# The steps of a forward substitution, written for VectorE and for GpSimd

## The chip, the cores and the metric

The kernel runs on one core of a Trainium2 chip. The metric is the device time of one execution in microseconds, and the median of the runs shown counts. Engines are named as the profile names them: PE (TensorE, with PEld for its weight loads), DVE (VectorE), ACT (ScalarE), POOL (GpSimd) and SP (SyncE, here a queue of DMAs).

## The reference

One layer of a hybrid decoder over 512 positions and 2048 channels. Half of the channels are 16 heads of a delta-rule recurrence, the other half pooled windows. Then follow an output projection, a gated embedding and a norm:

```python
h = rms_norm(x, norm_g[i])
z = jnp.einsum('btd,dn->btn', h, w_in[i])      # r, k, v, lora, gates, pool input
...
def step(S, inp):
    r_t, w_t, k_t, v_t, kk_t, a_t = inp
    sa = jnp.einsum('bhvk,bhk->bhv', S, -kk_t)
    S = (S * w_t[:, :, None, :]
         + sa[..., None] * (kk_t * a_t)[:, :, None, :]
         + v_t[..., None] * k_t[:, :, None, :])
    y_t = jnp.einsum('bhvk,bhk->bhv', S, r_t)
    return S, y_t
...
x = x + jnp.einsum('btc,cd->btd', y_mix, w_out[i])
gate = jax.nn.sigmoid(jnp.einsum('btd,de->bte', x, w_pg[i]) + b_pg[i])
x = x + gate * jnp.einsum('btq,qd->btd', p[i], w_ple[i])
```

All data is float32.

## The kernel before

Every large product is done three times with operands split into a high and a low part: a weight piece is loaded into `raw` by a DMA on SP's queue, ScalarE casts it to `whi`, VectorE subtracts to `wlo` (lines 127 to 134), and TensorE multiplies (`mm3`, line 164). There are four buffers of each, so a load can only start when the `wlo` of four pieces earlier is done, and SP issues its DMAs strictly in the order in which they stand on its queue.

The recurrence goes in eight pairs of heads (j = 0 to 7), and a pair's 512 positions in eight chunks of 64 (ch). Inside a chunk the recurrence is solved in closed form with a 64x64 triangular inverse, so that a pair's `recur(j)` is a chain of small products: `py` from the state `sbd`, `zs` on VectorE, `pu`, `uv` on ScalarE, `ps`, and the new state `sbd` on VectorE (lines 804 and 806). That last operation also adds `s0p`, the old state times the decay of the whole next chunk. It is prepared one chunk ahead on GpSimd (line 813), in two halves for the two heads, for the chunks 0 to 5. TensorE's order is the program's order in this part: between the small products stand matmuls of the input projections of the next pair (`pump`, 6, 9 and 9 of them around each chunk), so a small product that is late makes the matmuls behind it late too.

While pair j runs, `invert(j + 1)` works out the triangular inverses for the next pair by forward substitution: 31 steps, each a product into `tm` (line 657) and a sum into `xw` (line 661), both over all 128 partitions with (s // 4 + 1) x (31 - s) elements a partition, each reading what the one before wrote. Its input `n` comes through a store to DRAM, `nd`, and a load, both on SP's queue (lines 639 and 644). After the last step `xw` is stored to DRAM (`xd`, line 665), loaded back in another layout (`x1`, line 672), and `gather(j + 1)` transposes a part of it on VectorE (line 723), which a product `pq` on TensorE then uses.

`invert` is a generator. `recur` calls `step()` after the products of a chunk: twice in chunk 0 and three times in each chunk behind it, 23 hops in all. From the sixth hop on (the first one of chunk 2), each takes two steps of the generator, so the 31 steps end at the 21st hop, and the DMAs of `xd` follow there. The steps of a hop are tied by `tc.issue_after` behind an operation that the variable `lead` holds: the last `zs` or `sbd` on VectorE. For pair 0 there is no recurrence to run beside: `invert(0)` is run through at once, tied to nothing, and 130 matmuls (`HT`) are put behind it on TensorE before `gather(0)`. Apart from such ties a scheduler orders each engine's and each queue's instructions by its own estimate of when they can run.

Of the kernel before, what the change touches and what calls it, by code (L numbers as in the profile page):

```python
# [13 lines left out]
ALU = mybir.AluOpType  # L14

P = 128
# [18 lines left out]
def trunk_kernel(ctx: ExitStack, tc: tile.TileContext, x, p, norm_g, w_in, mu, w0, w_up, a0, a_up,  # L35
                 k_k, k_a, r_k, ln_w, ln_b, w_pool, pool_scale, w_out, w_ple, w_pg, b_pg, final_g, out):
    nc = tc.nc
# [118 lines left out]
    def mm(*a, **k):  # L156
        i = nc.tensor.matmul(*a, **k)  # L157
        return tc.keep_in_program_order(i) if pin[0] else i
# [34 lines left out]
    n_ = 0  # L193
# [298 lines left out]
    def pump(n):  # L492
        debt[0] += n
        while debt[0] > 0:
            c = next(big, None)
            if c is None:
                debt[0] = 0
                return
            debt[0] -= c
# [150 lines left out]
    def invert(j):  # L650
        nb = st_[j].pop("nb")
        xw = rw.tile([P, 8, 32], F32, name=f"xw{j}", tag="xw")
        tm = rw.tile([P, 8, 32], F32, name=f"tm{j}", tag="tm")
        for s in range(31):
            n_, w_ = s // 4 + 1, 31 - s
            xin = i32 if s == 0 else xw
            nc.vector.tensor_tensor(tm[:, 0:n_, 0:w_], xin[:, 0:n_, s:s + 1].to_broadcast([P, n_, w_]),
                                    nb[s // 16][:, s % 16:s % 16 + 1, s + 1:32].to_broadcast([P, n_, w_]), ALU.mult)
            if s == 0:
                nc.gpsimd.tensor_copy(xw, i32)  # L660
            nc.vector.tensor_tensor(xw[:, 0:n_, s + 1:32], xw[:, 0:n_, s + 1:32], tm[:, 0:n_, 0:w_], ALU.add)  # L661
            yield
        xd = dram.tile([2, 2, 8, 8, 4, 32], F32, name=f"xd{j}", tag="xd")
        for q in range(4):
            nc.sync.dma_start(out=xd[:, :, :, :, q, :].rearrange("a b u i c -> (a b u) i c"),
                              in_=xw[32 * q:32 * q + 32])
        x1 = rw.tile([P, 8, C], F32, name=f"x1{j}", tag="x1", bufs=2)
        nc.gpsimd.memset(x1, 0.0)
        for par in range(2):
            pb = 64 * (1 - par)  # L670
            for b in range(2):
                nc.sync.dma_start(out=x1[pb + 32 * b:pb + 32 * b + 32, :, 32 * b:32 * b + 32],
                                  in_=xd[par, b].rearrange("u i q c -> (i q) u c"))

        st_[j]["x1"] = x1
# [77 lines left out]
    def recur(j, work, between):  # L753
# [1 line left out]
        pw, ar, mt, bv, uv, bkn, mv, x1 = (d[n_] for n_ in ("pw", "ar", "mt", "bv", "uv", "bkn", "mv", "x1"))  # L755
        hop = [0]
        HC1, HC2, HC3 = HC
        lead = [None]


        def step():
            hop[0] += 1
            if hop[0] > HS:
                with tc.issue_after(lead[0].ins):
                    for _ in range(HN):
                        next(work, None)

# [3 lines left out]
        for ch in range(NCH):  # L771
            par, q = ch % 2, ch // 2
            pb = 64 * (1 - par)
            cur, nxt = sbd[ch % 2], sbd[(ch + 1) % 2]
            pcc = pw[:, ch, C:C + 1]
            sl = slice((ch % 4) * P, (ch % 4 + 1) * P)
            if ch % 4 == 0:
                py = psY.tile([P, T], F32, name=f"py{j}_{ch}", tag="y")
            zs = zsp[par]
            if ch > 0:  # L780
                mm(py[:, sl], ar[:, q, 2 * par:2 * par + 2, :], cur, start=ch in (1, 4), stop=True,
                                 skip_group_check=True)
                with tc.high_priority(offset=HP):
                    lead[0] = nc.vector.tensor_tensor(zs[pb:pb + 64], py[pb:pb + 64, sl], mv[pb:pb + 64, q, :],
                                                      ALU.add)
                step()
                pump(HC1)

            psu = psS.tile([P, T], F32, name=f"pu{j}_{ch}", tag="s")
            mm(psu[:, 0:P], x1[:, 2 * q:2 * q + 2, :], zs, start=True, stop=True)  # L790
            for h in range(2):
                hc = slice(64 * h, 64 * h + 64)
                with tc.high_priority(offset=HP):
                    nc.scalar.copy(uv[pb:pb + 64, ch, hc], psu[hc, hc])
            step()
            pump(HC2)
            if ch < NCH - 1:
                pss = psS.tile([P, T], F32, name=f"ps{j}_{ch}", tag="s")
                mm(pss[:, 0:P], bkn[:, ch, :], uv[:, ch, :], start=True, stop=True)
                for h in range(2):  # L800
                    hc = slice(64 * h, 64 * h + 64)
                    with tc.high_priority(offset=HP):
                        if ch == 0:
                            lead[0] = nc.vector.tensor_scalar(nxt[hc, hc], pss[hc, hc], pcc[hc], None, ALU.mult)
                        else:
                            lead[0] = nc.vector.scalar_tensor_tensor(nxt[hc, hc], pss[hc, hc], pcc[hc], s0p[hc, :],  # L806
                                                                     ALU.mult, ALU.add)
                s0p = rw.tile([P, C], F32, name=f"s0p{j}_{ch}", tag="s0p", bufs=2)
                pcn = pw[:, ch + 1, C:C + 1]
                if ch < NCH - 2:  # L810
                    for h in range(2):
                        hc = slice(64 * h, 64 * h + 64)
                        nc.gpsimd.tensor_scalar(s0p[hc, :], nxt[hc, hc], pcn[hc], None, ALU.mult)  # L813
            if ch % 4 == 3:
                for qq in range(2):
                    for h in range(2):
                        for pr in range(2):
                            c_ = ch - 3 + 2 * qq + pr
                            yr = slice(64 * pr, 64 * pr + 64)
                            o_ = (2 * qq + pr) * P + 64 * h  # L820
                            mm(py[yr, o_:o_ + 64], mt[:, pr, 2 * (c_ // 2) + h, pr, :],
                                             uv[:, c_, 64 * h:64 * h + 64], start=False, stop=True,
                                             skip_group_check=True)
                py4 = py.rearrange("p (s c) -> p s c", c=P)
                for pr in range(2):
                    yr = slice(64 * pr, 64 * pr + 64)
                    nc.scalar.copy(ysb[yr, q - 1:q + 1, :], py4[yr, pr::2, :])
            step()
            if ch == 0:
                between()  # L830
            else:
                pump(HC3)
# [48 lines left out]
    for _ in invert(0):  # L881
        pass
    pump(HT)
    gather(0)
    for j in range(NJ):
        def between():
            pump(H3 if j + 1 < NJ else HC[2])
            if j + 1 < NJ:
                scores(j + 1)
                pump_to(H2)  # L890

        if j + 1 == NJ:
            pn.append(rw.tile([P, NT, DPLE], F32, name="pn", tag="ar", bufs=2))
            for h in range(2):
                nc.scalar.dma_start(out=pn[0][:, 2 * h:2 * h + 2, :],
                                    in_=p[256 * h:256 * h + 256, :].rearrange("(t p) q -> p t q", p=P))
        if j + 1 < NJ:
            prepare(j + 1)
        recur(j, invert(j + 1) if j + 1 < NJ else iter(()), between)
        if j + 1 < NJ:  # L900
            gather(j + 1)
# [276 lines left out]
```

## Time and profile before

| | us |
|---|---|
| median of 3 runs | 1094.54 (1093.39 to 1097.44) |
| the profiled execution | 1094.06 |
| its span in the trace | 1092.3 |
| state product s0p on GpSimd, 96 | 56.7 in all |
| wlo_b on VectorE, 64 | 43.7 in all |

The span runs from the first to the last instruction; the profiled execution's own time lies a little above it. A group's line gives the line in the kernel, the engine, the operation, output and inputs, the count, then the time in all and the mean in ns, and behind the last bar the idle time of the engine ahead of it. A row of the timeline gives start, length, engine, line and operation, and in brackets how long the engine was idle before it and what ended that. In a row of a stretch's busy times stand the engines' busy microseconds with the number of instructions, then the granted clock of TensorE and the DMAs' share and rate. A wait's row says who waited for what, how long in all, how often, and the longest.

### The profile page before, as it was taken

The page shows a single profiled execution, that of the slowest core. Times are in us where ns is not written, and L with a number is a line of the kernel's source. Part 1 is how long each engine was busy: PE and PEld are TensorE (multiplying, and loading weights), DVE is VectorE, ACT ScalarE, POOL GpSimd, SP SyncE. Part 2 cuts the span into 40 slices and gives each one's busy share as a digit, 9 for nine tenths or more (in the row PEclk, how much of TensorE's full clock was granted, in tenths as well). Part 3 has the DMA queues.
Part 4 walks back from the last instruction along what each step waited for, and adds up shares of the span by engine and source line. Part 5 has one row for each costly group of instructions (what it writes and reads, how often), then busy time and mean ns, then how long its engine had stood idle before and what let it go on. Part 6 is the DMA issues. An engine that isn't in the chain of part 4 may idle for free.

```text
span 1092.3 us, 17194 instructions
## 1 busy us (share of the span) xinstructions
PE 1067.4 (98%) x6060; PEld 879.1 (80%) x6060; DVE 707.9 (65%) x1835; ACT 448.2 (41%) x917; POOL 74.4 (7%) x180
## 2 busy tenths in 40 slices
PE   5999999999999999999999999999999999999996
PEld 4888878888888888787888788888888888888885
DVE  6687867878779679678886956454433424445366
ACT  7633534435335335353443344544222222233337
POOL 2100010110110110100101101000000000000000
PEclk9999999999999999999999999999999999999999
DMA  7433433332423333333334242774534438454534
GB/s 233 116 97 97 112 92 79 102 101 72 127 81 102 105 91 89 95 83 90 94 93 120 79 138 94 231 242 163 171 123 141 164 97 261 129 187 147 174 105 154
DMA packets 178485, 138.56 MB, mean 127 GB/s; under 512 B 34677, under 2 KB 139742, under 8 KB 178398
## 3 DMA queue, kind: packets, MB, share of 16 engines
q1 hardware_dynamic: 157694, 103.89, 32.2%
q10 hardware_dynamic: 20704, 33.56, 9.5%
q8 instruction: 48, 0.79, 0.3%
q14 instruction: 39, 0.32, 0.1%
HBM read 118.02 MB, written 18.87 MB: 125 GB/s over the span
## 4 chain that ended last, share of the span: by engine, by line
PE 88%; DVE 5%; DMA 3%; ACT 2%; issue 1%; SPq 0%; ACTq 0%; DVEq 0%
PE acc_o L157 16%; PE acc_g L157 16%; PE zb L157 15%; PE zv L157 8%; PE zr L157 7%; PE zg L157 7%; PE zk L157 6%; DMA n<-nd 2%; PE py L157 2%; PE pple L157 2%; PE pu L157 2%; PE pm L157 1%; PE pp L157 1%; PE ps L157 1%; PE pmv L157 1%
## 5 line engine op out<-in xcount | busy, mean ns | idle before, releaser
L133 DVE TENSOR_TENSOR wlo_g<-raw_g,whi_g 128x512 fp32r<-128x512 f32 x84 | 56.9, 683 | 78.7 <-ACT whi_g L132 78.5
L157 PE MATMUL zb<-hhi,whi_b 128*128 128x512 f32 x256 | 106.3, 415 | 0.0
L133 DVE TENSOR_TENSOR wlo_o<-raw_o,whi_o 128x512 fp32r<-128x512 f32 x64 | 43.9, 690 | 92.3 <-ACT whi_o L132 92.2
L157 PE MATMUL zb<-hhi,wlo_b 128*128 128x512 f32 x256 | 100.5, 393 | 0.0
L157 PE MATMUL acc_o<-whi_o,ylo 128*128 128x512 f32 x256 | 100.2, 391 | 0.0
L157 PE MATMUL acc_o<-whi_o,yhi 128*128 128x512 f32 x256 | 99.9, 390 | 0.0
L157 PE MATMUL zb<-hlo,whi_b 128*128 128x512 f32 x256 | 99.8, 390 | 0.0
L157 PE MATMUL acc_o<-wlo_o,yhi 128*128 128x512 f32 x256 | 99.7, 389 | 0.0
L132 ACT CAST whi_g<-raw_g 128x512 fp32r<-128x512 f32 x84 | 51.9, 620 | 105.5 <-PE acc_g L157 60.3
L157 PE MATMUL acc_g<-whi_g,x2hi 128*128 128x512 f32 x208 | 81.2, 391 | 0.0
L157 PE MATMUL acc_g<-wlo_g,x2hi 128*128 128x512 f32 x208 | 81.0, 389 | 0.0
L157 PE MATMUL acc_g<-whi_g,x2lo 128*128 128x512 f32 x208 | 80.6, 389 | 0.0
L132 ACT CAST whi_o<-raw_o 128x512 fp32r<-128x512 f32 x64 | 39.9, 623 | 97.8 <-PE acc_o L157 97.8
L813 POOL TENSOR_SCALAR s0p<-sbd,pw 64x64 f32<-64x64 f32 x96 | 56.7, 590 | 338.5 <-DVE sbd L806 253.7
L132 ACT CAST whi_b<-raw_b 128x512 fp32r<-128x512 f32 x64 | 39.7, 620 | 87.1 <-PE zv L157 34.9
L133 DVE TENSOR_TENSOR wlo_b<-raw_b,whi_b 128x512 fp32r<-128x512 f32 x64 | 43.7, 684 | 34.2 <-ACT whi_b L132 33.0
L157 PEld LDWEIGHTS zb<-hhi,wlo_b 128*128 128x128 f32 x256 | 48.0, 188 | 11.0
L661 DVE TENSOR_TENSOR xw<-xw,tm 128x60 f32<-128x60 f32 (+24 forms) x248 | 51.9, 209 | 6.8
L157 PEld LDWEIGHTS acc_o<-wlo_o,yhi 128*128 128x128 f32 x256 | 48.1, 188 | 10.0
L157 PEld LDWEIGHTS acc_o<-whi_o,ylo 128*128 128x128 f32 x256 | 48.1, 188 | 9.9
L157 PEld LDWEIGHTS acc_o<-whi_o,yhi 128*128 128x128 f32 x256 | 48.1, 188 | 9.6
L157 PEld LDWEIGHTS zb<-hhi,whi_b 128*128 128x128 f32 x256 | 48.3, 189 | 8.4
(285 smaller groups left out, 2546.8 us busy)
## 6 DMA issues: line engine op xcount, KB each, us to landing
raw_b<-in_w_in_dram SPq DMA_DIRECT2D x64, 256.0 KB
raw_o<-in_w_out_dram SPq DMA_DIRECT2D x64, 256.0 KB
raw_g<-in_w_pg_dram SPq DMA_DIRECT2D x64, 256.0 KB
raw_k<-in_w_in_dram SPq DMA_DIRECT2D x32, 256.0 KB
raw_r<-in_w_in_dram SPq DMA_DIRECT2D x32, 256.0 KB
raw_v<-in_w_in_dram SPq DMA_DIRECT2D x32, 256.0 KB
raw_g<-in_w_in_dram SPq DMA_DIRECT2D x32, 256.0 KB
n<-nd SPq DMA_DIRECT2D x16, 256.0 KB
```

What stands on the lines that cost most here:

```text
L132: nc.scalar.copy(hi, raw)
L133: nc.vector.tensor_tensor(lo, raw, hi.bitcast(F32), ALU.subtract)
L157: i = nc.tensor.matmul(*a, **k)
L661: nc.vector.tensor_tensor(xw[:, 0:n_, s + 1:32], xw[:, 0:n_, s + 1:32], tm[:, 0:n_, 0:w_], ALU.add)
L813: nc.gpsimd.tensor_scalar(s0p[hc, :], nxt[hc, hc], pcn[hc], None, ALU.mult)
```

## The change

The two operations of a step are issued by GpSimd instead of VectorE. In `step()` the tie is another one: a new variable `held` holds the last s0p product (the second of the two halves), and the steps of a hop are put behind that instead of behind `lead`. `held` is set in the chunks 0 to 5, at the end of the chunk and ahead of its last hop. So at the first two hops of a chunk it is the s0p of the chunk before, at the last one that of the same chunk, and in the chunks 6 and 7 still that of chunk 5.

```diff
         for s in range(31):
             n_, w_ = s // 4 + 1, 31 - s
             xin = i32 if s == 0 else xw
-            nc.vector.tensor_tensor(tm[:, 0:n_, 0:w_], xin[:, 0:n_, s:s + 1].to_broadcast([P, n_, w_]),
+            nc.gpsimd.tensor_tensor(tm[:, 0:n_, 0:w_], xin[:, 0:n_, s:s + 1].to_broadcast([P, n_, w_]),
                                     nb[s // 16][:, s % 16:s % 16 + 1, s + 1:32].to_broadcast([P, n_, w_]), ALU.mult)
             if s == 0:
                 nc.gpsimd.tensor_copy(xw, i32)
-            nc.vector.tensor_tensor(xw[:, 0:n_, s + 1:32], xw[:, 0:n_, s + 1:32], tm[:, 0:n_, 0:w_], ALU.add)
+            nc.gpsimd.tensor_tensor(xw[:, 0:n_, s + 1:32], xw[:, 0:n_, s + 1:32], tm[:, 0:n_, 0:w_], ALU.add)
             yield
...
-        lead = [None]
+        lead, held = [None], [None]
...
         def step():
             hop[0] += 1
             if hop[0] > HS:
-                with tc.issue_after(lead[0].ins):
+                with tc.issue_after(held[0].ins):
                     for _ in range(HN):
                         next(work, None)
...
                 if ch < NCH - 2:
                     for h in range(2):
                         hc = slice(64 * h, 64 * h + 64)
-                        nc.gpsimd.tensor_scalar(s0p[hc, :], nxt[hc, hc], pcn[hc], None, ALU.mult)
+                        held[0] = nc.gpsimd.tensor_scalar(s0p[hc, :], nxt[hc, hc], pcn[hc], None, ALU.mult)
```

What this moves is seen in the engines' order. First GpSimd's queue in the recurrence of pair 0, chunks 1 and 2, with + for what is new there (s0p_1 and s0p_2 are the products of these chunks, tm and xw the tiles of the steps for pair 1):

```order
 L813 TENSOR_SCALAR s0p_1_1836<-sbd_566,pw_836 64x64 x2
+L660 COPY xw_1862<-i_116 128x256
+L657 TENSOR_TENSOR tm_1863<-i_116,n_0_1762 128x31
+L661 TENSOR_TENSOR xw_1862<-xw_1862,tm_1863 128x31
+L657 TENSOR_TENSOR tm_1863<-xw_1862,n_0_1762 128x30
+L661 TENSOR_TENSOR xw_1862<-xw_1862,tm_1863 128x30
+L657 TENSOR_TENSOR tm_1863<-xw_1862,n_0_1762 128x29
+L661 TENSOR_TENSOR xw_1862<-xw_1862,tm_1863 128x29
+L657 TENSOR_TENSOR tm_1863<-xw_1862,n_0_1762 128x28
+L661 TENSOR_TENSOR xw_1862<-xw_1862,tm_1863 128x28
 L813 TENSOR_SCALAR s0p_2_1908<-sbd_567,pw_836 64x64 x2
```

Before, the two products stood one behind the other. Now the copy and eight instructions of the steps stand between them; behind s0p_2, s0p_3 and s0p_4 stand twelve each, and behind s0p_5 the last eighteen. Second, VectorE's queue at the same place:

```order
 L784 TENSOR_TENSOR zs_568<-py_0_1664,mv_1612 64x128
-L657 TENSOR_TENSOR tm_1863<-i_116,n_0_1762 128x31
-L661 TENSOR_TENSOR xw_1862<-xw_1862,tm_1863 128x31
-L657 TENSOR_TENSOR tm_1863<-xw_1862,n_0_1762 128x30
-L661 TENSOR_TENSOR xw_1862<-xw_1862,tm_1863 128x30
-L657 TENSOR_TENSOR tm_1863<-xw_1862,n_0_1762 128x29
 L133 TENSOR_TENSOR wlo_k_2_1233<-raw_k_2_1230,whi_k_2_1232 128x512
-L661 TENSOR_TENSOR xw_1862<-xw_1862,tm_1863 128x29
-L657 TENSOR_TENSOR tm_1863<-xw_1862,n_0_1762 128x28
-L661 TENSOR_TENSOR xw_1862<-xw_1862,tm_1863 128x28
 L806 SCALAR_TENSOR_TENSOR sbd_567<-ps_2_1904,pw_836,s0p_1_1836 64x64 x2
```

The steps are gone from between zs, the weight split wlo_k and the state sbd, which stay in their order. Third, SP's queue behind the steps of pair 0 (raw_v and raw_b are weight pieces, xd the store of the steps' result, x its load into x1):

```order
 L129 DMA raw_v_2_943<-in_w_in_dram 128x4x128
+L665 DMA xd_1137<-xw_1072 256x1x32 x2
 L129 DMA raw_v_3_985<-in_w_in_dram 128x4x128
+L665 DMA xd_1137<-xw_1072 256x1x32 x2
 L129 DMA raw_b_0_991<-in_w_in_dram 128x4x128
+L672 DMA x_1142<-xd_1137 32x8x32 x2
 L129 DMA raw_b_1_1048<-in_w_in_dram 128x4x128
-L665 DMA xd_1137<-xw_1072 256x1x32 x2
+L672 DMA x_1142<-xd_1137 32x8x32 x2
 L129 DMA raw_b_2_1054<-in_w_in_dram 128x4x128
-L665 DMA xd_1137<-xw_1072 256x1x32 x2
 L129 DMA raw_b_3_1148<-in_w_in_dram 128x4x128
```

The stores of xd stand three weight pieces earlier, ahead of raw_v_3 and raw_b_0. The other pairs' stores stand one or two pieces earlier. The order on TensorE is the same as before.

## The prediction

> **What bounds the kernel now.** I read the page first, then the busy times of the stretch that holds the eight recurrences beside those of the stretch behind it, then the chain that ended last and the waits.
>
> ```profile
> span 1092.3 us, 17194 instructions
> PE 1067.4 (98%) x6060; PEld 879.1 (80%) x6060; DVE 707.9 (65%) x1835; ACT 448.2 (41%) x917; POOL 74.4 (7%) x180
> PE 88%; DVE 5%; DMA 3%; ACT 2%; issue 1%; SPq 0%; ACTq 0%; DVEq 0%
> core 0: us, PE busy (x) PEld busy (x) DVE busy (x) ACT busy (x) POOL busy (x), PEclk, DMA share, GB/s
> 77.00:692.00 615.00, 610.84 (x3916) 501.00 (x3913) 475.01 (x1403) 257.63 (x559) 64.98 (x115) 1.00 0.35 99
> DVE tm L657 <- DMA n<-nd: 18.3, 8, 3.8
> PEld py L157 <- DVE sbd L806: 5.9, 9, 1.0
> PEld pu L157 <- DVE zs L784: 3.4, 6, 0.9
> ```
>
> TensorE holds 88% of the last chain. In the 615 us of the recurrences it is busy for 610.84; VectorE for 475, or 77%; GpSimd for 65. So VectorE is well loaded, but it seldom makes TensorE wait: 5.9 us for the state sbd and 3.4 us for zs, together 9.3 us. That is about all that a lighter VectorE can win. The 18.3 us that VectorE itself stands idle for the tile n (eight times, once a pair) cost TensorE only what those 9.3 us hold. Against this stand places where the end of the 31 steps, or a state product s0p, decides when TensorE may go on. So the question is whether GpSimd does the steps soon enough.
>
> **What moves.** 62 instructions a pair, 496 in all, leave VectorE, where they took about 0.21 us each:
>
> ```profile
> L661 DVE TENSOR_TENSOR xw<-xw,tm 128x60 f32<-128x60 f32 (+24 forms) x248 | 51.9, 209 | 6.8
> L657 DVE TENSOR_TENSOR tm<-xw,n x240: 155/215/239, 89.7 to 628.3; 128x60 f32<-128x60 f32 x24, 128x28 f32<-128x28 f32 x16, 128x48 f32<-128x48 f32 x16, 128x30 f32<-128x30 f32 x8
> ```
>
> VectorE loses some 104 us of 708, hidden today under TensorE, so I count it as no gain beyond a share of the 9.3 us above. I take half of that, **-5 us**.
>
> **What a step costs on GpSimd.** No two-input operation runs there before. The nearest rows are the product s0p (64 elements a partition with a second operand, 435 ns at its shortest) and the mask selections (64 elements, one input: 1.2 us for 6, or 236 ns in the mean). The sizes compare: n_*w_ summed over the 31 steps is 1560 elements, 50 a step.
>
> ```profile
> L813 POOL TENSOR_SCALAR s0p<-sbd,pw x96: 435/447/2049, 129.2 to 687.5; 64x64 f32<-64x64 f32 x96
> L77 POOL TENSOR_SCALAR_AFFINE_SELECT msk<-msk 64x64 f32<-64x64 f32 x6 | 1.2, 236 | 0.1
> 217.86 0.97 POOL L813 TENSOR_SCALAR s0p<-sbd,pw 64x64 f32<-64x64 f32 x2 [10.05 <-DVE sbd L806]
> 163.27 1.33 POOL L813 TENSOR_SCALAR s0p<-sbd,pw 64x64 f32<-64x64 f32 x2 [5.71 <-DVE sbd L806]
> 163.53 0.69 DVE L133 TENSOR_TENSOR wlo_r<-raw_r,whi_r 128x512 fp32r<-128x512 f32 x1
> 205.76 2.05 POOL L813 TENSOR_SCALAR s0p<-sbd,pw 64x64 f32<-64x64 f32 x1
> 205.49 0.69 DVE L138 TENSOR_TENSOR kpl<-kp,kph 128x512 fp32r<-128x512 f32 x1
> 206.10 0.28 DVE L526 TENSOR_TENSOR as<-ar,as 64x128 fp32r<-64x128 f32 x1
> 206.30 0.68 DVE L133 TENSOR_TENSOR wlo_g<-raw_g,whi_g 128x512 fp32r<-128x512 f32 x1
> ```
>
> I take 0.33 us, about midway: a step has fewer elements than s0p, but reads two full inputs where the selection reads one. Both ends stay in the range, and a price under 0.236 isn't excluded, since VectorE needs 0.21. A pair of undisturbed s0p takes 0.97 us, 0.09 more than twice 0.44; each step's instruction reads what the one before wrote, so I add 0.09 for each: 0.42 us from one to the next, 62 x 0.42 = 26.0 us a pair.
>
> The last rows show a second price. An s0p pair takes 1.33 us instead of 0.97 when VectorE's wlo (two SBUF inputs) begins beside it, and an s0p met by kpl, as and wlo_g one behind the other takes 2.05 us. So GpSimd stands while VectorE runs such an instruction. Of these, wlo alone (its 7 and 10 instructions in two stretches) fills:
>
> ```profile
> 89.14:108.33 19.19, 4.19 (x7) 1.00 0.31 93
> 147.88:178.53 30.65, 6.90 (x10) 1.00 0.30 89
> ```
>
> That is 22% of both stretches (the steps of pairs 0 and 1), so GpSimd has 0.78 of its time.
>
> **Pair 0** has no recurrence beside it, and its steps are tied to nothing. The rows give the start and end of the steps, the store, the transpose of x1 and its first user pq on TensorE, and then the same start, end and user for pair 1:
>
> ```profile
> 89.14 0.19 DVE L657 TENSOR_TENSOR tm<-i,n 128x31 f32<-128x31 f32 x1 [3.75 <-DMA n<-nd]
> 108.15 0.18 DVE L661 TENSOR_TENSOR xw<-xw,tm 128x8 f32<-128x8 f32 x1
> 108.39 1.31 SPq L665 DMA_DIRECT2D xd<-xw  x2
> 116.83 0.89 DVE L723 STREAM_TRANSPOSE y<-x 32x256 f32<-32x256 f32 x2
> 120.90 0.69 PE L157 MATMUL pq<-y,mt 32*32 32x32 f32 x32
> 147.88 0.19 DVE L657 TENSOR_TENSOR tm<-i,n 128x31 f32<-128x31 f32 x1 [2.85 <-DMA n<-nd]
> 178.35 0.18 DVE L661 TENSOR_TENSOR xw<-xw,tm 128x8 f32<-128x8 f32 x1
> 195.40 0.69 PE L157 MATMUL pq<-y,mt 32*32 32x32 f32 x32
> ```
>
> On GpSimd 26.0 / 0.78 = 33.3 us, so the steps end at 122.5 instead of 108.3: 14.2 late. From the last step over both DMAs to the end of the transpose are 117.72 - 108.33 = 9.4 us, and pq came at 120.90, so 3.2 us are free. **Cost 11 us.** On SP's queue the last v weights of this pair now stand behind the first stores of xd; they come late with them and wait inside the same 11 us.
>
> **Pairs 1 to 6.** Between the n tile and the end GpSimd now does 62 step instructions and the eight s0p of chunks 2 to 5: 26.0 + 8 x 0.53 = 30.3, over 0.78 is 38.8 us, against 30.65 on VectorE: 8.2 late. Free are 195.40 - 178.53 - 9.4 = 7.5 us: 0.7 short. The second deadline is s0p itself, because what is queued behind a waiting step is now the next chunk's s0p, for which VectorE's sbd waits, and behind sbd the weight splits:
>
> ```profile
> 150.58 1.30 POOL L813 TENSOR_SCALAR s0p<-sbd,pw 64x64 f32<-64x64 f32 x2 [6.43 <-DVE sbd L806]
> 169.48 1.31 POOL L813 TENSOR_SCALAR s0p<-sbd,pw 64x64 f32<-64x64 f32 x2 [4.88 <-DVE sbd L806]
> ```
>
> Three chunks between them make 6.3 us a chunk. GpSimd needs (12 x 0.42 + 2 x 0.53) / 0.78 = 7.8 us, so it falls back by 1.5 a chunk. The first eight step instructions end at 147.88 + 8 x 0.42 / 0.78 = 152.2, 1.6 behind 150.58; three chunks later it is 6.1 behind. A product is wanted one chunk after it can begin, less its own 1.06 / 0.78: 4.9. So 1.2 short. Both shortfalls are one stall, of about 1.2: **7 us for six pairs**. Pair 7 has pooling sums beside its steps, which also read two inputs; the rows are pairs 1 and 7 over all engines:
>
> ```profile
> 147.88:178.53 30.65, 30.24 (x158) 24.53 (x157) 25.39 (x99) 11.51 (x25) 5.01 (x9) 1.00 0.30 89
> 596.91:628.73 31.82, 31.44 (x163) 25.09 (x161) 29.08 (x114) 10.49 (x24) 5.81 (x8) 1.00 0.28 83
> ```
>
> VectorE is busy for 29.08 us there against 25.39, 3.7 more, in which GpSimd stands too: with the 1.2 of the other pairs **5 us**.
>
> **Sum**: 11 + 7 + 5 - 5 = +18. The profiled execution took 1094.06 (its span 1092.3 and 1.8 around it; the median is 1094.54, so the execution stands for it): **1112 us**.
>
> **The rivals.**
>
> *GpSimd becomes the bound of every pair.* At s0p's 0.435 the pitch is 0.525. Pair 0: 32.6 / 0.78 = 41.7, 22.5 late, cost 19. Each other pair: (32.6 + 4.2) / 0.78 = 47.1, 16.5 late, 9 over the free 7.5; six make 54, pair 7 some 11, minus 5: +79, **1173 us**. For it speaks that s0p is the only arithmetic measured there under the same neighbours; against it, that copies of 256 elements over all partitions took 667 ns in the mean, so 50 elements should be well under that.
>
> ```profile
> L660 POOL COPY xw<-i 128x256 f32<-128x256 f32 x8 | 5.3, 667 | 195.4 <-PE px L157 195.4
> ```
>
> The Trainium skill, GPSIMD Engine Reference, section Engine selection, speaks against the change: two-input elementwise work is about twice as slow there as on VectorE. Twice VectorE's 0.21 would be an estimate of 0.42 us and so this rival; no run here shows it.
>
> *It is hidden.* At the selections' 0.236 the pitch is 0.326: pair 0 takes 25.9 us, 6.7 late, cost 3.5; a later pair ends (20.2 + 4.2) / 0.78 = 31.3 after its start, 0.6 late of 7.5 free, and a chunk needs 6.4 us of 6.3. Sum 3.5 - 5: **1093 us**, no change.
>
> *VectorE's relief wins, the other side.* If a step takes 0.21 us or less, or GpSimd gets at its data between VectorE's instructions, even pair 0 ends within its 3.2 us. Then only the 9.3 us of waits for sbd and zs are in play: **1085 us**. It decides from a pitch below (19.2 + 3.2) x 0.78 / 62 = 0.28 us. Against it speaks that no GpSimd arithmetic on 64 elements is under 0.236.
>
> **How the numbers follow.** A measurement of this kernel tells about 0.5% (5.5 us) from no change. The forecast, with a price of some 0.28 to 0.38 us and +6 to +45, gets 0.45; GpSimd bound in every pair 0.27; hidden 0.18; relief 0.10. So faster 0.10, same 0.18, slower 0.72. The range goes from 1090, leaving out most of the relief, to 1165, leaving out the worst part of the bound case.
>
> **What would show it.** In the profile after: L657 and L661 on POOL with a mean near 0.33 us and longer where a wlo runs; steps of pair 0 ending near 122 and pq of pair 0 some 11 us later than now; s0p of chunk 5 starting 5 us or more behind its sbd; sbd L806 on VectorE waiting for POOL s0p; py waiting for sbd by far more than 5.9 us. The forecast is wrong if a step's price is under 0.25 (nothing waits) or over 0.4 (each pair stretches by some 9 us from the 74.5 between the first two pq), or if the 0.22 share of the shutting out does not hold once GpSimd asks all the time.

## The result, and the profile after

The changed kernel takes **1129.93 us** (median of 5 runs, 1129.5 to 1134.98) against 1094.67 us before (5 runs, 1093.39 to 1097.44): a ratio of 1.033 with an interval from 1.0304 to 1.0356. It is 35.3 us slower, where 18 were forecast. The profiled execution took 1134.98 us, 40.9 us more than the profiled one of before; the sums below are made against that, and what the 5 us between the profiled execution and the median are comes out at the end of the experiments.

The page after:

```profile
span 1133.3 us, 17210 instructions
...
PE 1080.3 (95%) x6060; PEld 890.4 (79%) x6060; DVE 618.7 (55%) x1339; ACT 447.6 (39%) x917; POOL 232.6 (21%) x676
...
PE 80%; POOL 9%; DMA 3%; ACT 2%; issue 2%; DVE 2%; SPq 1%; ACTq 0%; POOLq 0%; DVEq 0%
```

VectorE has lost 89 us of work, GpSimd gained 158, and GpSimd now holds 9% of the chain that ended last, where it had no place before. TensorE is busy for 13 us more although it does the same 6060 instructions: part of them ran slower.

Where the time went is read from the start of the first pq of each pair, and from the distance to the next pair's. The table has before, after and five experiments that are told below; behind pq of pair 7 before and after take 447.1 us alike.

| us | pair 0 at | to 1 | to 2 | to 3 | to 4 | to 5 | to 6 | to 7 |
|---|---|---|---|---|---|---|---|---|
| before | 120.90 | 74.50 | 74.21 | 74.94 | 75.44 | 73.85 | 76.55 | 74.83 |
| after | 134.24 | 73.58 | 77.88 | 80.75 | 79.02 | 77.90 | 80.08 | 82.72 |
| e1_n_elsewhere | 133.76 | 73.58 | 73.99 | 73.67 | 74.93 | 72.33 | 76.32 | 82.26 |
| e2_first_dve | 121.23 | 73.59 | 75.58 | 78.93 | 77.46 | 77.94 | 78.08 | 81.70 |
| e3_both | 120.55 | 73.58 | 74.03 | 73.64 | 74.93 | 72.35 | 76.39 | 81.46 |
| e8_pool_queue | 124.72 | 77.78 | 73.97 | 73.65 | 74.92 | 72.48 | 76.34 | 83.88 |
| e9_middle_pairs | 121.35 | 73.58 | 73.98 | 73.68 | 74.92 | 72.34 | 76.33 | 74.55 |

So pair 0 costs 13.3 us, pairs 2 to 6 together 20.6, pair 7 7.9, and pair 1 gives 0.9 back. Three different places lie behind that. These are the waits after (who waited for whom, us in all, times, longest):

```profile
ACT kk L557 <- POOL tm L657: 30.1, 6, 7.4
...
PE ps L157 <- ACT uv L794: 12.3, 4, 4.4
...
PE pbk L161 <- ACT sig L532: 10.7, 1, 10.7
...
PE pyt L161 <- DVE ysb L851: 5.2, 1, 5.2
...
PE py L157 <- DVE sbd L806: 2.8, 2, 2.0
```

None of the four waits of TensorE (the rows of PE) is for pq, and only the last one is for the state sbd.

**Pair 0.** Two rows of the timeline before, the loads of raw_v and the cast of the last of them:

```profile
91.61 9.32 SPq L129 DMA_DIRECT2D raw_v<-in_w_in_dram  x4
...
105.16 0.62 ACT L132 CAST whi_v<-raw_v 128x512 fp32r<-128x512 f32 x1 [0.99 <-PE zr L157]
```

The timeline after, from the last step on:

```profile
114.30 0.22 POOL L661 TENSOR_TENSOR xw<-xw,tm 128x8 f32<-128x8 f32 x1
114.55 1.31 SPq L665 DMA_DIRECT2D xd<-xw  x2
115.97 0.54 SPq L129 DMA_DIRECT2D raw_v<-in_w_in_dram  x1
...
119.19 0.62 ACT L132 CAST whi_v<-raw_v 128x512 fp32r<-128x512 f32 x1 [14.44 <-DMA raw_v<-in_w_in_dram]
...
121.77 0.68 ACT L532 ACTIVATE sig<-pu,dprm 128x512 f32<-128x512 f32 x1
...
122.51 1.12 PE L161 MATMUL pbk<-ident,bk 128*128 128x128 f32 x4 [10.72 <-ACT sig L532]
```

The store of xd stands on SP's queue and waits for the last step until 114.55. Behind it stands the last load of raw_v, which before had gone out by 100.93; so ScalarE waits 14.44 us for it with the cast whi_v. Behind that cast stands sig, which belongs to the next pair's decay and reads the product pu out of one of three buffers that TensorE's results take in turn. The transposes pbk need that buffer, and so TensorE waits 10.72 us for sig. No link of this chain behind the store reads what the steps compute.

**Pairs 2 to 6.** The timeline of pair 2, while the steps for pair 3 run (the table's column "to 3"):

```profile
328.30 0.30 POOL L657 TENSOR_TENSOR tm<-xw,n 128x64 f32<-128x64 f32 x1
...
328.63 0.72 ACT L557 ACTIVATE kk<-sk,prm 128x512 f32<-128x512 f32 x1 [7.44 <-POOL tm L657]
...
330.40 0.42 ACT L794 COPY uv<-pu 64x64 f32<-64x64 f32 x2
...
330.88 0.80 PE L157 MATMUL ps<-uv,bkn 128*128 128x128 f32 x2 [4.43 <-ACT uv L794]
```

The first half of n (steps 0 to 15) lies in the buffer that kk has too (line 643). ScalarE's square kk for pair 4, the pair after the one whose steps run, may only be written when step 15 has read n; the product with 64 elements at 328.30 is that read. ScalarE waits 7.44 us, and behind kk on its queue stands uv of the running recurrence, for which TensorE waits 4.43 us. The wait of 2.0 us for sbd, one pair earlier, comes the same way through VectorE: kk waits 2.71 us there, VectorE waits 4.34 us to split it, and sbd stands behind that split.

The buffer bound kk before the change too:

```profile
309.98 0.23 DVE L657 TENSOR_TENSOR tm<-xw,n 128x64 f32<-128x64 f32 x1
...
310.29 0.72 ACT L557 ACTIVATE kk<-sk,prm 128x512 f32<-128x512 f32 x1 [0.84 <-ACT uv L794]
```

kk began 0.08 us after the same read had ended, here and in three more pairs. ScalarE had stood idle for no more than 0.84 us by then, though, and TensorE waited for no uv.

**Pair 7.** The timeline at the end of pair 6, before and after:

```profile
638.03 0.44 DVE L723 STREAM_TRANSPOSE y<-x 32x256 f32<-32x256 f32 x1 [0.96 <-DMA x<-xd]
...
639.46 1.64 DVE L851 TENSOR_SCALAR ysb<-ysb,mvr,rs 128x64 f32<-128x64 f32 x7
```

```profile
675.58 0.43 DVE L723 STREAM_TRANSPOSE y<-x 32x256 f32<-32x256 f32 x1 [7.48 <-DMA x<-xd]
...
679.03 1.87 DVE L851 TENSOR_SCALAR ysb<-ysb,mvr,rs 128x64 f32<-128x64 f32 x8
...
679.61 1.81 PE L161 MATMUL pyt<-ident,ysb 128*128 128x128 f32 x4 [5.16 <-DVE ysb L851]
```

VectorE waits 7.48 us at the transpose of x1, with the group norm of pair 6 (ysb) queued behind it, and TensorE waits 5.16 us for that with the transposes pyt. Before, x1 was already the last to come, by 0.96 us, and most of the norm stood ahead of the first transpose or, as the row of ysb, ahead of the second at 641.03.

**The clock.** Six microseconds behind each of the seven stalls (the 12.3 us are four of them, the 2.0 one more), with TensorE's busy time in the first column behind the stretch's length and the granted clock behind POOL's column:

```profile
122.50:128.50 6.00, 5.99 (x18) 4.92 (x19) 5.41 (x10) 5.00 (x11) 0.00 (x0) 0.55 0.62 165
253.06:259.06 6.00, 6.00 (x22) 4.96 (x23) 1.36 (x3) 1.03 (x3) 4.96 (x14) 0.72 0.31 87
330.87:336.87 6.00, 5.99 (x18) 4.91 (x19) 1.76 (x5) 0.89 (x2) 3.55 (x10) 0.56 0.32 91
410.80:416.80 6.00, 6.00 (x22) 4.92 (x23) 3.08 (x7) 1.91 (x3) 3.55 (x10) 0.72 0.15 44
488.70:494.70 6.00, 6.00 (x22) 4.97 (x23) 2.98 (x7) 1.89 (x3) 4.14 (x11) 0.72 0.30 87
567.05:573.05 6.00, 6.00 (x22) 4.96 (x23) 2.27 (x6) 1.21 (x2) 3.69 (x9) 0.72 0.07 22
679.61:685.61 6.00, 5.93 (x17) 4.30 (x18) 3.96 (x10) 1.40 (x2) 0.00 (x0) 0.61 0.42 131
```

The clock falls short of 1 by 0.45 + 0.28 + 0.44 + 0.28 + 0.28 + 0.28 + 0.39 = 2.40 in the sum, times 6 us: 14.4 us. The stalls themselves are 10.7 + 12.3 + 2.0 + 5.2 = 30.2 us. Together 44.6; less the 4.7 us by which pairs 1 to 6 run shorter than before where nothing stalls (the table's row e9 against the row of before), 39.9 of the 40.9 us. So in this execution each stall is paid a second time by a TensorE that runs at a lower clock behind it.

### The profile page after: what moved, and what is told of

Its sections match the earlier page's. It is cut to its first block, busy times and chain, and to the rows that moved or that the text cites. A ratio compares the mean times of both kernels' runs of the same rounds, so it can differ in the third digit from the quotient of the medians.

```text
span 1133.3 us, 17210 instructions
## 1 busy us (share of the span) xinstructions
PE 1080.3 (95%) x6060; PEld 890.4 (79%) x6060; DVE 618.7 (55%) x1339; ACT 447.6 (39%) x917; POOL 232.6 (21%) x676
## 4 chain that ended last, share of the span: by engine, by line
PE 80%; POOL 9%; DMA 3%; ACT 2%; issue 2%; DVE 2%; SPq 1%; ACTq 0%; POOLq 0%; DVEq 0%
PE acc_o L157 15%; PE acc_g L157 15%; PE zb L157 13%; PE zv L157 8%; PE zg L157 7%; PE zk L157 5%; PE zr L157 4%; POOL xw L661 4%; POOL tm L657 4%; PE pple L157 1%; PE py L157 1%; PE pm L157 1%; PE pu L157 1%; DMA n<-nd 1%; POOL s0p L813 1%
## 5 line engine op out<-in xcount | busy, mean ns | idle before, releaser
L813 POOL TENSOR_SCALAR s0p<-sbd,pw 64x64 f32<-64x64 f32 x96 | 54.0, 562 | 351.4 <-DVE sbd L804 222.3
L661 POOL TENSOR_TENSOR xw<-xw,tm 128x60 f32<-128x60 f32 (+24 forms) x248 | 82.5, 333 | 18.9
L657 POOL TENSOR_TENSOR tm<-xw,n 128x60 f32<-128x60 f32 (+10 forms) x240 | 79.3, 330 | 18.9
L132 ACT CAST whi_o<-raw_o 128x512 fp32r<-128x512 f32 x64 | 39.9, 623 | 98.0 <-PE acc_o L157 97.7
```

Source lines behind the costliest of these rows:

```text
L132: nc.scalar.copy(hi, raw)
L657: nc.gpsimd.tensor_tensor(tm[:, 0:n_, 0:w_], xin[:, 0:n_, s:s + 1].to_broadcast([P, n_, w_]), nb[s // 16][:, s % 16:s % 16 + 1, s + 1:32]. ...
L661: nc.gpsimd.tensor_tensor(xw[:, 0:n_, s + 1:32], xw[:, 0:n_, s + 1:32], tm[:, 0:n_, 0:w_], ALU.add)
L813: held[0] = nc.gpsimd.tensor_scalar(s0p[hc, :], nxt[hc, hc], pcn[hc], None, ALU.mult)
```

## The experiments

Two theories stood after the first profile. K: in pairs 2 to 6 the buffer that n and kk share is what costs, through ScalarE's queue. Q: in pair 0 it is the order of SP's queue. The rival to both is the prediction's own account, F: s0p late in each chunk, and x1 late in pair 0.

**n elsewhere.** The changed kernel, with the first half of n in a buffer that ScalarE's kk doesn't use:

```diff
-            t_ = rw.tile([P, 16, 32], F32, name=f"n32{j}_{i}", tag=("kk", "kp")[i])
+            t_ = rw.tile([P, 16, 32], F32, name=f"n32{j}_{i}", tag=("ipw", "kp")[i])
```

> The changed kernel, but the first half of the tile n lies in the buffer of ipw instead of that of kk, so ScalarE's square kk for the pair after the next no longer waits until step 15 has read n. Theory K: in pairs 2 to 6 (3.7, 5.8, 3.6, 4.1 and 3.5 us longer than before, 20.7 in all) it is this wait on ScalarE, with the copies uv of the recurrence queued behind it, that stops TensorE: the five pairs lose at least 17 us of that, and the time goes from 1129.9 to about 1110 to 1113. Theory F, as forecast: the state products s0p and the late end of the steps do it; then n's place is without effect and the time stays within 1127 to 1131.

Measured: 1109.55 us (1107.99 to 1109.65), ratio 1.013 [1.0105, 1.0156], 20.4 us less than the changed kernel. The table's row shows where: pairs 2 to 6 are now at or below before, pairs 0 and 7 as after the change. Its waits:

```profile
PE pbk L161 <- ACT sig L532: 10.3, 1, 10.3
...
PE pyt L161 <- DVE ysb L851: 5.3, 1, 5.3
...
ACT kk L557 <- DVE sk L370: 4.0, 4, 1.3
```

kk waits for no step any more, and the wait of ps for uv is gone. GpSimd does as much as after the change (busy for 238 us, 233 there) and s0p stands behind as many steps, so in these pairs F falls and K is shown.

**Pair 0's steps on VectorE.** The two operations are issued by VectorE for j = 0 alone; in the second kernel n lies elsewhere as well:

```diff
+        eng = nc.vector if j == 0 else nc.gpsimd
...
-            nc.gpsimd.tensor_tensor(tm[:, 0:n_, 0:w_], xin[:, 0:n_, s:s + 1].to_broadcast([P, n_, w_]),
+            eng.tensor_tensor(tm[:, 0:n_, 0:w_], xin[:, 0:n_, s:s + 1].to_broadcast([P, n_, w_]),
...
-            nc.gpsimd.tensor_tensor(xw[:, 0:n_, s + 1:32], xw[:, 0:n_, s + 1:32], tm[:, 0:n_, 0:w_], ALU.add)
+            eng.tensor_tensor(xw[:, 0:n_, s + 1:32], xw[:, 0:n_, s + 1:32], tm[:, 0:n_, 0:w_], ALU.add)
```

> The changed kernel, but the 62 step instructions of pair 0 alone go back to VectorE; those of pairs 1 to 7 stay on GpSimd. In the changed kernel pq of pair 0 comes 13.3 us later than before. If that is all pair 0's steps, the time falls by 12 to 14 us, to 1116 to 1118. If part of it comes from elsewhere (the scheduler's other order, GpSimd in general), it falls by less than 10.

> Both edits: pair 0's steps on VectorE and n in ipw's buffer. If the two costs are separate and add, 1129.9 less 12 to 14 less 17 to 20, so 1096 to 1101, with the 7.9 us of pair 7 left and no gain from a lighter VectorE. If the lighter VectorE is worth the 5 us that the forecast counted, 1091 to 1096. Theory F: 1114 to 1118, as pair 0 alone.

Measured: 1116.76 us (ratio 1.02 [1.0172, 1.0227]), 13.2 less than after, pair 0's own 13.3; and both edits 1097.06 us (10 runs, ratio 1.0018 [1.0009, 1.0027]). The two gains, 20.4 and 13.2, add up to 33.6; both together give 32.9. What is still lost against before is pair 7, whose distance is 6.6 us longer, against 4.6 us that pairs 1 to 6 run shorter.

**Is it the order of SP's queue in pair 0?** In the first kernel the stores of pair 0 are put behind the last weight piece raw_b_3, so that raw_v goes first:

```diff
-    for _ in invert(0):
-        pass
+    inv0 = invert(0)
+    for _ in range(31):
+        next(inv0)
...
+    with tc.issue_after(wload["b0_3"].ins):
+        next(inv0, None)
```

> The changed kernel, all steps on GpSimd, but the store and load of pair 0's result stand behind the weight piece raw_b_3 on SP's queue instead of ahead of raw_v_3. Theory Q: pair 0's loss is the weight load raw_v_3 that stands behind the store on SP's queue (ScalarE waited 14.4 us for it, and TensorE 11 for ScalarE): the stall goes and the time falls by 9 to 12 us, to 1118 to 1121, with up to 3 left because x1 comes 6 us later than before and only 3.2 were free. Theory F, as forecast: the loss is the late x1 itself; then the time stays within 1127 to 1131 or falls by 3 at most.

Measured: 1131.69 us, ratio 1.0323 [1.0282, 1.0364]: nothing gained. pbk doesn't wait any more, but pq does, twice, as the timeline of its fastest execution shows, 1123.95 us (its line numbers are two higher than in the changed kernel):

```profile
125.08 0.43 DVE L725 STREAM_TRANSPOSE y<-x 32x256 f32<-32x256 f32 x1 [4.00 <-DMA x<-xd]
...
125.66 0.28 PE L159 MATMUL pq<-y,mt 32*32 32x32 f32 x2 [4.33 <-DVE y L725]
...
131.10 1.06 PE L159 MATMUL pq<-y,mt 32*32 32x32 f32 x30 [5.15 <-DVE y L725]
```

The second kernel removes the order without delaying the stores: n elsewhere, and the stores of xd and loads of x1 of all pairs on GpSimd's own queue.

```diff
-            nc.sync.dma_start(out=xd[:, :, :, :, q, :].rearrange("a b u i c -> (a b u) i c"),
+            nc.gpsimd.dma_start(out=xd[:, :, :, :, q, :].rearrange("a b u i c -> (a b u) i c"),
...
-                nc.sync.dma_start(out=x1[pb + 32 * b:pb + 32 * b + 32, :, 32 * b:32 * b + 32],
+                nc.gpsimd.dma_start(out=x1[pb + 32 * b:pb + 32 * b + 32, :, 32 * b:32 * b + 32],
```

> The steps stay on GpSimd; the first half of n lies in the other buffer as in the first experiment (1109.55), and the stores of xd and the loads of x1 go through GpSimd's own queue, so that no weight piece on SP stands behind a store that waits for the steps. If the order of SP's queue is what costs pair 0 its 13 us and pair 7 its 8, both go: 1090 to 1098. If the late end of the steps itself costs them (x1 late at the product pq, as the run with the late store suggests), pair 0 keeps some 5 to 9 and pair 7 most of its 7: 1100 to 1108. If issuing DMAs on GpSimd delays its s0p products, it is slower than 1109.55.

Measured: 1106.83 us, ratio 1.0107 [1.0082, 1.0133], 2.7 less than with n elsewhere alone. Its timeline at pq of pair 0, and the busy times of the stretch behind it:

```profile
123.67 0.90 DVE L723 STREAM_TRANSPOSE y<-x 32x256 f32<-32x256 f32 x2 [4.18 <-DMA x<-xd]
...
124.72 1.06 PE L157 MATMUL pq<-y,mt 32*32 32x32 f32 x32 [3.92 <-DVE y L723]
```

```profile
124.72:133.89 9.17, 9.17 (x108) 7.77 (x109) 9.17 (x11) 3.53 (x8) 0.00 (x0) 0.50 0.20 59
```

Without weight pieces behind the stores, the first wait of TensorE is that for x1, 3.92 us; then it runs for at least 9.17 us at half the clock, which costs 4.6. Together 8.5: pq of pair 1 stands at 202.50 against 194.13 in the kernel with both edits, 8.4 later. The steps end at 115.74 there, 7.4 later than before, and by the prediction 3.2 us of that are free. With SP's order and n elsewhere pq of pair 1 stood at 207.34. So of 13.2 us in pair 0 some 4.8 hang on the order of SP's queue, and 8.4 are left in the best order tried, by the late end of the steps and the clock behind it. Q is right for where the changed kernel waits, and wrong for what is won by mending it; F, in the sense of a late x1, holds for the greater part of pair 0. Pair 7 keeps all of its loss (83.88 in the table), so the order of SP's queue is not what costs it.

**The middle pairs alone.** Pairs 0 and 7 on VectorE (for 7 with the old tie behind lead), pairs 1 to 6 on GpSimd, n elsewhere:

```diff
+        eng = nc.vector if j in (0, NJ - 1) else nc.gpsimd
...
-                with tc.issue_after(held[0].ins):
+                with tc.issue_after((lead if j == NJ - 2 else held)[0].ins):
```

> Pairs 1 to 6 on GpSimd, n in ipw's buffer; the steps of pairs 0 and 7 on VectorE, pair 7's tied behind zs and sbd as before. With pair 0 alone back and n moved, 1097.1 was measured, with pair 7 still 6.6 us longer than before and the five pairs from pq of pair 1 on together 4.6 us shorter. If the end of pair 7's steps is what costs there, those 6.6 go: 1089 to 1092, faster than before by 3 to 6 us. If pair 7's loss has another cause, it stays near 1097.

Measured: **1089.66 us** (1089.32 to 1091.63), ratio 0.9955 [0.9943, 0.9967]: 0.5% faster than before. At the end of pair 6 the norm stands ahead of the second transpose again, and pyt doesn't wait:

```profile
633.35 0.44 DVE L724 STREAM_TRANSPOSE y<-x 32x256 f32<-32x256 f32 x1 [0.77 <-DMA x<-xd]
...
636.75 0.60 PE L161 MATMUL pyt<-ident,ysb 128*128 128x128 f32 x4
```

Two controls belong to it. The kernel before, with n elsewhere and nothing else:

> The kernel before, all steps on VectorE, with n in ipw's buffer alone. It tells whether the 4.6 us that the middle pairs won come from a VectorE without the steps or from n's new place. From the lighter VectorE: this stays within 1093 to 1097. From n's place: 1089 to 1092.

Measured: 1093.21 us (12 runs), ratio 0.9984 [0.9976, 0.9993]: n's place alone is worth 1.9 of the 5.5 us, which leaves 3.6 for a VectorE without the steps of the middle pairs. And the changed kernel with the steps 1 to 30 left out in every pair, so that neither engine has them:

> Steps 1 to 30 of every pair are left out, so that neither VectorE nor GpSimd has more than two of the 62 instructions of a pair; the end of the steps can no longer be late. This is what the relief of VectorE can bring at most. Forecast of the prediction: 5 to 9.3 us under before's 1095, so 1085 to 1090. If n's place costs something by itself, 2 us less. A result at 1080 or below would say that the steps on VectorE held TensorE up by more than the waits for sbd and zs show.

Measured: 1089.05 us, ratio 0.9947 [0.9926, 0.9968], 5.5 us under the before of the same runs. Without the late steps n is also read early, so n's place counts in here as well. The middle pairs on GpSimd already get about as much as leaving the steps out altogether.

**The tie.** The changed kernel with the steps tied behind lead, as before:

```diff
-                with tc.issue_after(held[0].ins):
+                with tc.issue_after(lead[0].ins):
```

> The changed kernel with one part undone: the steps on GpSimd are tied behind zs and sbd as before and not behind s0p. The scheduler then puts s0p of chunk 2 behind about 40 step instructions and those of chunks 3 to 5 behind all 62, where 8 and 12 stood. At 0.40 us each the product of chunk 3 comes some 12 us late in each of seven pairs: if the order behind s0p decides, 1200 to 1240. If s0p has room enough, or the tie does nothing, 1128 to 1134.

Measured: 1192.38 us, ratio 1.0897 [1.0876, 1.0918]. Its waits are those that the prediction had named:

```profile
DVE sbd L806 <- POOL s0p L813: 72.6, 25, 10.2
...
PE py L157 <- DVE sbd L806: 54.7, 11, 10.3
```

So F exists, and the new tie takes it away: s0p is put ahead of the steps of its hop, and 62 us less are lost. The other half of the change alone, the steps on VectorE tied behind held:

> The other part alone: all steps on VectorE, tied behind s0p. The order puts 8 to 24 step instructions ahead of a state sbd that the recurrence waits for, where 2 to 8 stood; at 0.25 us each that is 2 to 4 us a chunk in four chunks of seven pairs. If this order costs what it says, 1130 to 1190; if the state has room for it, 1094 to 1100.

Measured: 1126.38 us, ratio 1.0292 [1.0279, 1.0306]. Here VectorE's timeline shows the steps standing ahead of zs:

```profile
227.28 0.19 DVE L657 TENSOR_TENSOR tm<-i,n 128x31 f32<-128x31 f32 x1 [4.06 <-DMA n<-nd]
...
229.14 0.30 DVE L784 TENSOR_TENSOR zs<-py,mv 64x128 f32<-64x128 f32 x1
...
229.49 0.51 PE L157 MATMUL pu<-zs,x 128*128 128x128 f32 x2 [3.37 <-DVE zs L784]
```

The first step waits for the load of n, zs stands behind it and the three steps that follow, and TensorE waits for zs. So of the four pairings of engine and tie, all with n in kk's buffer, the one before is the fastest, and on GpSimd the new tie is the better one by 62 us.

**The clock, in a second profile.** The changed kernel and the one with the late store, unaltered, each profiled again:

> The changed kernel itself, unaltered, profiled a second time, to see whether TensorE's stalls and the granted clock behind them account for its time. In the first profiled execution (1134.98) the waits of TensorE that are new in the recurrences sum to 30.2 us, and the clock was 0.5 to 0.7 behind every one of the seven, 14.4 us lost by it. If the clock is a second price, decided anew in each execution behind the stalls of 2 to 4 us, the waits come out again at 29 to 31 us, and the time differs from 1134.98 by the difference in what the clock takes, to within 1.5 us: near the median of 1130 some 9 to 10 us lost, with full clock behind two or three of the shorter stalls. If the clock has nothing to do with it, the waits themselves are shorter in a faster execution, by as much as the time is.

> The kernel with the late store, unaltered, profiled a second time. Its first profile was of its fastest execution (1123.95, the others 1131.19 to 1133.17), with full clock behind four of the five stalls of 1.4 to 3.1 us in the middle pairs. If the clock is decided anew in each execution, an execution near 1131 shows the same waits, and the clock at 0.5 to 0.75 behind most of these stalls, some 7 us more lost by it. If the clock has nothing to do with it, the waits are longer by 7 us.

Measured: 1130.25 us and 1129.0 us. The changed kernel's stalls sum to 28.1 us here (10.5 + 10.9 + 2.4 + 4.3), a little less than expected, and behind two of the short ones the clock is full:

```profile
329.49:335.49 6.00, 6.00 (x29) 5.05 (x30) 2.45 (x6) 1.63 (x4) 3.89 (x9) 1.00 0.35 98
406.64:412.64 6.00, 6.00 (x29) 5.04 (x30) 3.13 (x7) 2.72 (x6) 3.55 (x10) 1.00 0.30 85
```

Of the 4.7 us that it is faster than in the first profile, 2.1 are shorter stalls; the clock takes 11.2 us, summed over TensorE's busy time, instead of 14.4, which is 3.2 more (together 5.3, 0.6 too many). The late store shows it more plainly, first in the execution of 1123.95 us, then in that of 1129.0:

```profile
326.82:332.82 6.00, 6.00 (x29) 5.05 (x30) 2.44 (x6) 1.63 (x4) 3.91 (x9) 1.00 0.34 98
```

```profile
326.60:332.60 6.00, 6.00 (x16) 4.93 (x17) 1.76 (x5) 0.64 (x2) 3.56 (x10) 0.50 0.32 91
```

At the same place of the program TensorE does 29 matmuls in 6 us in the one and 16 in the other. The second execution took 5.05 us more with stalls that sum to 1.6 us less (24.2 instead of 25.8); the clock took 15.4 us in it instead of 7.6. The stalls don't explain the difference between executions, the clock does. The five executions that gave the result fit this too: their times fall with the mean granted clock, from 1134.98 us at 0.980 over 1131.72 at 0.981 and 1129.93 at 0.983 to 1129.5 at 0.987.

## Why the prediction was right in direction and short in size

The sum was 11 for pair 0, 7 for pairs 1 to 6, 5 for pair 7 and -5 for the relief. In the profiled execution, counted by stalls and the clock behind them, the terms are 13.4, 23.7, 7.5 and -4.7. Two steps of the prediction failed: in pairs 1 to 6 the mechanism, a state product s0p that falls behind, and behind every stall the missing price of the clock. A third, the weights of pair 0 that would wait inside the same 11 us, is told with that pair.

**The price of a step** was met in the mean only, and then used wrongly. The groups after:

```profile
L661 POOL TENSOR_TENSOR xw<-xw,tm 128x60 f32<-128x60 f32 (+24 forms) x248 | 82.5, 333 | 18.9
L657 POOL TENSOR_TENSOR tm<-xw,n 128x60 f32<-128x60 f32 (+10 forms) x240 | 79.3, 330 | 18.9
```

0.33 us was forecast for a step that VectorE leaves alone, and 333 and 330 ns are measured. But that mean already holds the time in which VectorE keeps GpSimd out: the medians are 0.298 and 0.292 us, and single steps are far longer, as in the timeline of pair 2, where VectorE's wlo_r runs from 319.95 to 320.62:

```profile
319.99 0.77 POOL L657 TENSOR_TENSOR tm<-xw,n 128x50 f32<-128x50 f32 x1
320.84 0.28 POOL L661 TENSOR_TENSOR xw<-xw,tm 128x50 f32<-128x50 f32 x1
```

So the agreement of the two numbers is luck. The 62 instructions of pair 0 took from 89.80 to 114.52, 24.7 us or 0.40 each, where 33.3 were forecast; those for pair 1 took 30.5, not 38.8. At the median and the 0.08 us between two of them they would be some 0.37 apart (an estimate from these rows), so VectorE took about 7% of GpSimd's time in pair 0 and not 22%. The prediction's estimate by the Trainium skill (GPSIMD Engine Reference, Engine selection) was twice VectorE's time for two inputs. Here the mean is 1.6 times VectorE's (0.333 / 0.209).

**Pair 0, 11 us forecast, 13.3 measured: the size nearly right by errors that cancel.** The steps end 6.2 us late, not 14.2, which by the prediction's own free 3.2 us would have cost 3. The step that failed is the sentence that the v weights behind the first stores "wait inside the same 11 us": the wait for them through whi_v, sig and pbk, 10.72 us, is the one that TensorE meets, and it leaves a slow clock behind. The order of SP's queue had been seen and quoted; what was behind raw_v on ScalarE's queue had not been followed.

**Pairs 1 to 6, 7 us forecast, 23.7 measured ahead of the relief: the mechanism failed.** The prediction let s0p fall behind by 1.5 us a chunk. After the change VectorE's sbd waits for GpSimd for 6.0 us in all, and TensorE's py for sbd for 2.8, of which 2.0 are kk's doing. s0p is not what costs, since the steps are cheaper than forecast and the new tie keeps s0p ahead of them; with the old tie it would have been, as the run shows. What was missed is that a slower reader holds the buffer longer: kk and n share one, which line 643 says, and its next writer stands on ScalarE ahead of uv. Stalls of 14.3 us come of it, and 9.4 of the clock behind them. That the loss hangs on this buffer is shown by moving n: 20.4 us gone, where the same move gives 1.9 in the kernel before.

**Pair 7, 5 us forecast, 7.9 measured: the mechanism half right.** The pooling sums do stretch the steps, as forecast. In the kernel with n elsewhere, where pairs 1 to 6 lose nothing, the steps take 35.1 us for pair 7 and 30.9 for pair 6, and 19 of the 62 instructions are longer than 0.45 us instead of 9; nine of the 19 run beside the pooling work of lines 417 to 421. On VectorE, before, pair 7's took only 0.8 us more than pair 6's. But the prediction let the late end cost TensorE directly. What TensorE waits for is the norm of pair 6, queued behind the transpose that waits for x1. That the norm alone, put ahead of the transposes with the steps still on GpSimd, would mend it was not tried; taking the pair's steps off GpSimd does.

**The relief of VectorE, -5 us forecast,** came out near that, in part by luck: 3.6 us beside the kernel with n elsewhere alone, 5.5 at the most. The 9.3 us of which half was taken are waits of weight loads (the rows of PEld). TensorE's products themselves waited 1.9 us for sbd and 0.7 for zs before. The opposite rival needed all of the 9.3 and no stall; the middle-pairs kernel has no stall and wins 5.5, n's place included.

**A term that the sum had not:** the clock behind each stall, 14.4 us in the profiled execution. It is why stalls of 30 us became 45. The true stalls of 2 to 11 us met it. The forecast's stall of 1.2 us a pair would hardly have: behind two of 1.4 us in the executions with the late store the clock was full.

## What to carry to other kernels

When work moves to a slower engine, follow not only who needs its result but every buffer that it reads until later and every queue on which an instruction waits for it: the price is set by what stands behind the waiting instruction, here uv behind kk, sig behind whi_v, the norm behind a transpose, none of which uses the steps. Move a part only where its end has slack: the six middle pairs together gained on GpSimd once n no longer shared kk's buffer. The first, with 3.2 us free, and the last, whose transpose already waited for x1 before, lost 13 and 7 us. And price a stall of TensorE in a dense stretch at its length and 1 to 2 us more, which is what the clock took per stall in the four executions above.

## What the runs showed of the hardware

The granted clock falls behind stalls of two microseconds already, though not each time. Behind 10.72 us of idling it was 0.55 over the next 6 us, behind 4.43 us 0.56, and behind one of 1.86 us 0.72 in the one execution; in the other, stalls of 3.39 and 1.86 us were followed by the full clock. The rows of two matmuls of the same shape after the change show what it does:

```profile
123.85 0.63 PE L157 MATMUL zv<-hlo,whi_v 128*128 128x512 f32 x1
...
128.25 0.39 PE L157 MATMUL zv<-hlo,whi_v 128*128 128x512 f32 x1
```

The Trainium skill, TensorE: Matmul & The Clock Gate, section What's actually happening, has the clock halved after an idle window of about 3.4 us and full again after about as long a busy one, with windows that run freely. The half clock agrees with the granted 0.50 of two stretches above, and the chance in it with the two executions; that an idle time of 1.86 us can do is less than that figure. The return to full took more than 9.17 us in the kernel with its stores on GpSimd's queue, whose first products behind the stall are small (32x32 and 64x64), against some 5 behind the stall of pair 0 after the change (0.55 in the mean of the 6 us behind it); whether their size is the reason was not tried.
